# Blocks of head outputs in four tiles of their own, loaded inside the gates; second projection weights ahead in the load queue; bias rows copied from tile to tile

## The chip, the cores and the metric

One core of a Trainium2 chip runs the whole program. The metric is device time in microseconds; the time before is the median of three runs, 2127.23 us (2127.11 to 2127.78). A profiled execution of the same kernel has its own time, 2127.56 us, and its own span, 2125.8 us; the span is what the profile divides up.

## The reference

Two layers (DEPTH = 2) over 512 tokens of width 1024, all float32. In each layer one input projection feeds two branches, dilated window attention (output `y_a`, 384 wide) and retention (output `y_b`, 2048 wide: 4 heads of 512). The two are projected and merged by sigmoid gates, projected again, and followed by a SwiGLU feed-forward part; each sublayer ends in a layer norm.

```python
y_b = (jax.nn.silu(g_r) * y_r.reshape(B, S, RET_V_WIDTH)).astype(x.dtype)
merged = (jax.nn.sigmoid(gate_a) * jnp.einsum('bsc,cd->bsd', y_a, w_attn_proj)
          + jax.nn.sigmoid(gate_b) * jnp.einsum('bsc,cd->bsd', y_b, w_ret_proj))
return jnp.einsum('bsd,de->bse', merged, w_out)
```

## The kernel before

**Products.** Every float32 matrix is split into a high part (a cast on ScalarE, ACT) and a low part (the difference, on VectorE, DVE); `hilo` (L94) does both, `unit` (L123) does it for a weight tile of 128 x 1024, and a product is three matmuls: high by high, high by low, low by high. A matmul here streams 512 columns. Large products use seven block products instead of eight (`ORDER`, L313: A11·B11, A12·B21, S1·P1, S4·B22, S2·P2, S3·P3, A22·P4), where the S are sums of blocks of the left operand, split in the tile `xs`, and the P sums of weight blocks. A block product is 24 matmuls: two token tiles of 12.

**Loads.** Weights are loaded by `load` (L110) through the DMA queue of SyncE (SP) into one of eight shared buffers of 4 KB per partition, `raw` (L98); a buffer is free again when its two halves have been split. SP issues in order: a load that waits for a buffer holds up all loads behind it. Additions done by a DMA, and some loads and stores, go through GpSimd's (POOL's) queue, also in order.

**Order of work.** The program is written in one order, with a list `side` of small jobs handed out by `tick` between matmuls. The compiler then plans each engine's queue: an instruction written later can be put ahead of an earlier one on its engine when by the planner's own reckoning its inputs are ready first. On the chip each queue runs in that planned order, and an instruction that waits holds what stands behind it.

**The stretch that the change touches**, once per layer:
1. The last retention head's outputs are transposed and stored to DRAM as `y_d` (`turn`, L1038).
2. `gates(0)` and `gates(1)` (L1088) are two products of the layer's input with the gate weights: `left` makes `sga` tiles, `right` writes a sigmoid into a buffer `sb` (two of them) and stores it to `g_d`. The first block product of a chain is copied out of PSUM by ACT (`sn`, L496) before the next accumulates onto it.
3. During `gates(1)`, from its third block product, `side` holds `ya_put` (splits the attention output `yaT`) and `y_block` (loads two of the four blocks of `y_d`, heads 0 and 1, into `raw` buffers).
4. `was`: four weight units of the attention projection. Then `y_put` splits blocks (0, 0) and (0, 1) of `y_d` into `xh` and `xl`, the tiles that held the layer's input, and the two other blocks are loaded. `b11` is the first pair of weight tiles of the second (retention) projection.
5. Eight groups of nine matmuls are the attention projection; each is multiplied by its gate (`sg`, L1142) and stored to `g_d` by POOL. From the third group on the list `more` hands out `y_put(1, 1)` and the four sums `x_sums` (L208), which are done in place in the `y_d` blocks.
6. The retention projection (L1188 on): heads 0 and 1 by block products (`product`, L1213), heads 2 and 3 by plain ones (`plain`, L1223), four rounds of 24 matmuls with a weight tile each. The order is A11, A12, plain 0 to 3, S1 and so on. Four loads `yq` bring heads 2 and 3 from `y_d`; three are split into the tile `yp`, the fourth into a quarter of `xh` that is free. `u21` is the weight pair of A12. `p1` holds the sum B11 + B12: `p_load` loads the one and POOL adds the other (L1206).

**Memory.** Stage pools are stacked from two sides. On the right, after the shared buffers, stand `yap` (10 KB per partition: `yaT`, `cos`, `sin`) and later, in its place, `fin` (8 KB, the residual tile `xtok`) and `pp` (8 KB, `p1`); on the left stand the nine slots `opp` (36 KB) and `ret` (the retention tiles and `sb`), and later `m` (32 KB) and `yp` (24 KB). A tile waits for the last use of the tiles whose bytes it takes over.

At the very start, `bias_rows` (L462) gathers bias rows of both layers into a tile `rb`, twice: rows 0 to 15 and rows 32 to 47 hold the same values; the second copy becomes the low part.

Of the kernel before, what the change touches and what calls it, by code (L numbers as in the profile page):

```python
# [11 lines left out]
F32 = mybir.dt.float32  # L12
# [7 lines left out]
P = 128  # L20
S = 512
D = 1024
KD = D // P
NI = S // P
DEPTH = 2
# [30 lines left out]
def hybrid_kernel(ctx, tc, x, rel_bias, w_in, b_in, w_attn_proj, w_ret_proj, w_out,  # L56
# [23 lines left out]
    def stage(name, bufs=1, side="left"):  # L80
        return tc.tile_pool(name=name, bufs=bufs, side=side, reuse_waits="tile")
# [28 lines left out]
    def load(src, a, b):  # L110
        v = view(raw(), a, b)
        for v_, s_ in pieces(v, src):
            nc.sync.dma_start(v_, s_)
        return v
# [8 lines left out]
    def unit(v):  # L123
        a, b = v.shape[1], v.shape[2]
        h = view(wp.tile([P, 1024], F32R, tag="whi", name="whi"), a, b)
        l = view(wp.tile([P, 1024], F32R, tag="wlo", name="wlo"), a, b)
        hilo(v, h, l)
        return h, l
# [36 lines left out]
    def pace(us):  # L165
        rate[0], credit[0] = len(side) / us, 0.0

    def drain():
        while side:
            side.popleft()()  # L170
# [37 lines left out]
    def x_sums(cp):  # L208

        (a11, a12), (a21, a22) = cp  # L210

        def one(n, o_, a, b, op):
            dve.tensor_tensor(out=o_, in0=a, in1=b, op=op)  # L213
            t = xs[:, SN.index(n)]
            hilo(o_, t[:, 0], t[:, 1])

        return [lambda a=a: one(*a) for a in (("S1", a22, a21, a22, ALU.subtract), ("S3", a21, a11, a21, ALU.subtract),
                                              ("S2", a22, a22, a11, ALU.subtract), ("S4", a22, a22, a12, ALU.add))]
# [237 lines left out]
    def va_row(ly, t):  # L456
        return DEPTH * RH + 2 * ly + t

    def gate_row(ly, t):
        return DEPTH * (RH + 2) + 2 * ly + t  # L460

    def bias_rows():  # L462


        r = raw("rb")
        pool.memset(r, 0.0)
        for q in (0, BK):
            for ly in range(DEPTH):
                for b2 in range(2):
                    o, e = b2 * RV, (C_VR, C_GR)[b2]  # L470
                    pool.dma_start(r[q + ly * RH:q + (ly + 1) * RH, o:o + RV],
                                   b_in[ly, e:e + RH * RV].rearrange("(h n) -> h n", h=RH))
                    e = C_VA + 2 * b2 * VB
                    pool.dma_start(r[q + va_row(ly, 0):q + va_row(ly, 2), o:o + VB],
                                   b_in[ly, e:e + 2 * VB].rearrange("(h n) -> h n", h=2))
                    e = (C_GA, C_GB)[b2]
                    pool.dma_start(r[q + gate_row(ly, 0):q + gate_row(ly, 2), o:o + S],
                                   b_in[ly, e:e + D].rearrange("(h n) -> h n", h=2))

        def make():  # L480
            dve.tensor_tensor(out=r[:, RV:], in0=r[:, RV:], in1=r[:, :RV], op=ALU.add)
            act.copy(out=bh, in_=r)
            e = slice(BK, 2 * BK)
            dve.tensor_tensor(out=bh[e], in0=r[e], in1=bh[e].bitcast(F32), op=ALU.subtract)

        return make
# [197 lines left out]
    def layer(ly, cp):  # L684
# [6 lines left out]

        heads = [{} for _ in range(RH)]
        lay = ExitStack()
        yap = lay.enter_context(stage("yap", side="right"))
        yaT = yap.tile([P, NG, S], F32, name="yaT")
        opp = lay.enter_context(stage("opp", 9))
        csp = yap
# [294 lines left out]
                next(vg)  # L992
            drain()

        with stage("ret") as rp:
            def ret_scores(h):

                dec = rp.tile([P, S], F32, tag="dec", name="dec")
# [74 lines left out]
            wa_l, wr_l = rows(w_attn_proj[ly]), rows(w_ret_proj[ly])  # L1073
            y_v = rows(y_d)
            sga, ya, yb = [None] * NI, [], [[None, None], [None, None]]

            def ya_put(t):
                ya.append(slot("ya"))
                hilo(yaT[:, t], ya[t][:, 0], ya[t][:, 1])

            def y_block(a, b):
                yb[a][b] = load(y_v[:, 4 * b:4 * b + 4, a * 256:a * 256 + 256], 4, 256)

            def y_put(a, b):
                ks, ts_ = slice(4 * b, 4 * b + 4), slice(a * 256, a * 256 + 256)
                hilo(yb[a][b], xh[:, ks, ts_], xl[:, ks, ts_])

            def gates(c):  # L1088

                cs = slice(c * S, (c + 1) * S)  # L1090

                def left(i, ps, s):
                    if s is not None:
                        dve.tensor_tensor(out=s, in0=ps, in1=s, op=ALU.add)
                    if sga[i] is None:
                        sga[i] = slot("sg", F32)
                    act.activation(out=sga[i][:, c], in_=ps if s is None else s, func=AF.Sigmoid)

                def right(i, t):
                    sb = rp.tile([P, S], F32, tag="sb", name="sb", bufs=2)  # L1100
                    act.activation(out=sb, in_=t, func=AF.Sigmoid)
                    act.dma_start(g_d[1, i * P:(i + 1) * P, cs], sb)

                return biased(halves(w_l, 0, (2, 2), C_GA + c * S, C_GB + c * S, S), S, gate_row(ly, c), left, right)
# [3 lines left out]
            for n_, _ in enumerate(gates(1)):  # L1108
                if n_ == 2:
                    drain()  # L1110
                    side.extend([nothing] * 4 + [lambda t=t: ya_put(t) for t in range(NG)] + [lambda b=b: y_block(0, b) for b in range(2)])
                    pace(18)
            drain()

            def block_w(b, u):
                k = 4 * (b[1] == "2") + 2 * u
                c = (b[2] == "2") * S
                return wr_l[:, k:k + 2, c:c + S]
# [2 lines left out]
                return wr_l[:, 2 * RH + 2 * u:2 * RH + 2 * u + 2, hf * S:(hf + 1) * S]  # L1121

            was = [[unit(load(wa_l[:, o:o + n, hf * S:(hf + 1) * S], n, S)) for o, n in ((0, 2), (2, 1))] for hf in range(2)]
            for b in range(2):
                y_put(0, b)
            for b in range(2):
                y_block(1, b)
            more = [lambda: y_put(1, 1)] + x_sums(yb)
            b11 = [load(block_w("B11", u), 2, S) for u in range(2)]
            for hf in range(2):  # L1130
                if hf:
                    u11 = [unit(r) for r in b11]
                for i in range(NI):
                    ps = psum("ps")
                    ks = [(u, k) for u in was[hf] for k in range(u[0].shape[1])]
                    for t, ((h, l), k) in enumerate(ks):
                        yh, yl = (ya[t][:, e, i * P:(i + 1) * P] for e in range(2))
                        mm(ps, yh, h[:, k], t == 0, False)
                        mm(ps, yh, l[:, k], False, False)
                        mm(ps, yl, h[:, k], False, t == NG - 1)  # L1140
                    v = sga[i][:, hf]
                    dve.tensor_tensor(out=v, in0=v, in1=ps, op=ALU.mult)  # L1142
                    pool.dma_start(g_d[0, i * P:(i + 1) * P, hf * S:(hf + 1) * S], v)
                    if hf * NI + i >= 2 and more:
                        more.pop(0)()
        lay.close()

        fin = ExitStack()
        fp = fin.enter_context(stage("fin", side="right"))
        xt = [fp.tile([P, 2, D], F32, name="xtok")]  # L1150
        res = (x if ly == 0 else spill).rearrange("(h i p) d -> h p i d", p=P, h=2)
        pool.dma_start(xt[0], res[0])

        def xtok(i):
            return xt[i // 2][:, i % 2]
# [32 lines left out]
        with stage("mp") as mp:  # L1188
# [4 lines left out]
            with stage("yp") as ypp, stage("pp", side="right") as ppp:  # L1193
# [66 lines left out]
                        act.copy(out=t, in_=ps)  # L1260
                    return ts

                yq = [load(y_v[:, 8 + 2 * q:10 + 2 * q], 2, S) for q in range(4)]
                u21 = [unit(load(block_w("B21", u), 2, S)) for u in range(2)]
                while more:
                    more.pop(0)()
                for q, r in enumerate(yq[:3]):
                    hilo(r, yp[:, 0, 2 * q:2 * q + 2], yp[:, 1, 2 * q:2 * q + 2])
                hilo(yq[3].rearrange("p e (h t) -> p (e h) t", h=2), xh[:, 0:4, 256:S], xl[:, 0:4, 256:S])
                for u in range(2):  # L1270
                    p_load(u, "B11", False)
                for u in range(2):
                    p_load(u, "B12", True)

                A = pair()
                product("A11", u11, A, True)
                ahead = unit(load(plain_w(0, 0), 2, S))
                sn1 = copies(A)
                X = pair()
                product("A12", u21, X, True)  # L1280
                Y = pair()
                for u in range(4):
                    now = ahead
                    if u < 3:
                        ahead = unit(load(plain_w(u + 1, 0), 2, S))
                    else:
                        for i in range(2):
                            g_load(i, 0)
                        ahead = p_units()
                    plain(u, now, X + Y)  # L1290
# [28 lines left out]
                    dve.tensor_tensor(out=sn5[a], in0=sn5[a], in1=Z[a], op=ALU.add)  # L1319
                now, ahead = ahead, [unit(r) for r in p3]  # L1320
                product("S2", now, A, False)
                sn6 = copies(A)
                for a in range(2):
                    dve.tensor_tensor(out=sn6[a], in0=C[a], in1=sn6[a], op=ALU.subtract)
# [251 lines left out]
```

## Time and profile before

| what | us |
|---|---|
| median of three runs | 2127.23 |
| profiled execution: its time / its span | 2127.56 / 2125.8 |
| TensorE (PE) busy in the span | 2091.5 |
| layer 0: last matmul of A11 / first of A12 | 590.56 / 595.64 |
| layer 1: last matmul of A11 / first of A12 | 1645.13 / 1650.52 |

In the lists below a timeline row is: start, duration, engine, line, operation, tiles written and read, shapes, and in brackets the idle time of that engine just before with what ended it. A row of waits is: engine, tile and line that waited, what it waited for, then microseconds in total, how many times, and the longest. A row of DMA issues ends in the KB of one transfer and the median us from issue to landing. A row of stretches gives, after its window, the busy time of PE, weight loads, DVE, ACT and POOL, then the granted PE clock, the share of the DMA engines' time and GB/s.

### The profile page before, as it was taken

How to read it: one execution, taken by the hardware profiler on the slowest of the kernel's cores; microseconds unless marked ns; L12 is line 12 of the kernel's file. 1: busy time of each engine (PE TensorE's matmuls, PEld its weight loads, DVE VectorE, ACT ScalarE, POOL GpSimd, SP SyncE). 2: the span in 40 equal slices, each digit the busy share in tenths (PEclk: the TensorE clock that was granted, in tenths of full speed). 3: DMA queues.
4: the chain of work that ended last, by engine and by line, in shares of the span. 5: the costliest groups of instructions: out<-in, count | busy, mean ns of one | idle time of the engine just before them, and what ended most of it. 6: DMA issues, size and time to landing. Idle time of an engine off the chain costs nothing. (4 is left out here: it accounts for less than half of the span.)

```text
span 2125.8 us, 33803 instructions
## 1 busy us (share of the span) xinstructions
PE 2091.5 (98%) x13178; PEld 1867.7 (88%) x13178; DVE 1623.9 (76%) x2327; ACT 1129.2 (53%) x1725; POOL 285.6 (13%) x299
## 2 busy tenths in 40 slices
PE   8999999999989999999999999999999999999998
PEld 7989888888778898999899898888887789989897
DVE  7666888786756698887787578887766567988876
ACT  5567655555543265555355765555654433655551
POOL 4111111110110101111030111111001111110111
PEclk9999999999999999999999999999999999999999
DMA  7866567676887458868258555758667873687771
GB/s 231 214 172 142 135 150 183 178 181 164 242 254 231 113 140 201 195 156 231 80 156 221 151 126 135 193 136 216 165 178 246 252 225 79 162 198 186 183 198 46
DMA packets 303905, 374.37 MB, mean 176 GB/s; under 512 B 23277, under 2 KB 208785, under 8 KB 303616
## 3 DMA queue, kind: packets, MB, share of 16 engines
q1 hardware_dynamic: 213056, 259.30, 39.5%
q0 software_dynamic: 63280, 100.11, 25.3%
q10 hardware_dynamic: 27408, 12.80, 2.1%
q8 instruction: 103, 1.69, 0.3%
q14 instruction: 58, 0.48, 0.1%
HBM read 346.36 MB, written 28.53 MB: 176 GB/s over the span
## 5 line engine op out<-in xcount | busy, mean ns | idle before, releaser
L351 DVE TENSOR_TENSOR wlo<-raw,whi 128x1024 fp32r<-128x1024 f32 (+1 forms) x518 | 605.0, 1171 | 200.5 <-ACT whi L345 186.3
L345 ACT CAST whi<-raw 128x1024 fp32r<-128x1024 f32 (+1 forms) x518 | 519.8, 1007 | 442.2 <-PE ps L84 188.9
L84 PE MATMUL ps<-xs,whi 128*128 128x256 f32 x2176 | 399.5, 284 | 0.4 <-ACT sn L813 0.4
L84 PE MATMUL ps<-whi,xs 128*128 128x512 f32 (+1 forms) x1152 | 348.2, 372 | 5.7 <-ACT sn L496 5.7
L84 PEld LDWEIGHTS ps<-xs,whi 128*128 128x128 f32 x2176 | 339.4, 192 | 4.9 <-issue 1.7
L84 PE MATMUL ps<-xh,whi 128*128 128x256 f32 (+1 forms) x1104 | 318.4, 290 | 2.2 <-ACT xh L95 1.9
L84 PE MATMUL ps<-xl,whi 128*128 128x256 f32 (+1 forms) x1104 | 315.5, 286 | 0.0
L84 PE MATMUL ps<-xh,wlo 128*128 128x256 f32 (+1 forms) x1104 | 315.1, 286 | 0.0
L84 PE MATMUL ps<-xs,wlo 128*128 128x256 f32 x1088 | 308.0, 283 | 2.6 <-DVE wlo L351 2.6
L84 PEld LDWEIGHTS ps<-whi,xs 128*128 128x128 f32 x1152 | 209.9, 188 | 40.8 <-ACT sn L496 6.8
L84 PEld LDWEIGHTS ps<-xh,whi 128*128 128x128 f32 x1104 | 210.4, 191 | 10.2 <-ACT xh L95 3.4
L84 PEld LDWEIGHTS ps<-xl,whi 128*128 128x128 f32 x1104 | 211.4, 192 | 3.0 <-DVE xl L96 0.6
L84 PE MATMUL ps<-wlo,xs 128*128 128x512 f32 (+1 forms) x576 | 212.9, 370 | 0.1
L84 PEld LDWEIGHTS ps<-xh,wlo 128*128 128x128 f32 x1104 | 211.2, 191 | 1.5
L84 PEld LDWEIGHTS ps<-xs,wlo 128*128 128x128 f32 x1088 | 208.5, 192 | 3.2 <-DVE wlo L351 3.2
L336 POOL DMA_DIRECT2D raw<-in_w_in x80 | 97.4, 1239 | 692.3 <-DMA raw<-in_w_in 290.6
L84 PE MATMUL ps<-whi,xh 128*128 128x512 f32 (+1 forms) x464 | 177.2, 382 | 9.7 <-ACT whi L95 9.7
L367 DVE TENSOR_TENSOR raw<-raw 128x1024 f32<-128x1024 f32 (+1 forms) x148 | 173.9, 1175 | 6.9 <-DMA raw<-in_w_in 4.9
L84 PE MATMUL ps<-wlo,xh 128*128 128x512 f32 (+1 forms) x464 | 174.3, 376 | 1.4 <-DVE wlo L96 1.4
L84 PE MATMUL ps<-whi,xl 128*128 128x512 f32 (+1 forms) x464 | 173.8, 375 | 0.0
L84 PE MATMUL ps<-whi,ht 128*128 128x512 f32 x544 | 170.1, 391 | 0.0
L95 ACT CAST whi<-raw 128x1024 fp32r<-128x1024 f32 (+1 forms) x78 | 76.0, 983 | 108.7 <-PE ps L84 79.6
(241 smaller groups left out, 3322.9 us busy)
## 6 DMA issues: line engine op xcount, KB each, us to landing
raw<-in_w_in SPq DMA_DIRECT2D x168, 512.0 KB, 5.2
raw<-in_w_in POOLq DMA_DIRECT2D x64, 512.0 KB, 8.7
raw<-in_w_ffn_up SPq DMA_DIRECT2D x64, 512.0 KB, 4.9
raw<-in_w_ffn_down SPq DMA_DIRECT2D x52, 512.0 KB, 4.7
raw<-in_w_ffn_gate SPq DMA_DIRECT2D x44, 512.0 KB, 4.9
raw<-in_w_ffn_gate POOLq DMA_DIRECT2D x40, 512.0 KB, 7.5
raw<-in_w_ret_proj SPq DMA_DIRECT2D x32, 512.0 KB, 5.9
raw<-in_w_in SPq DMA_DIRECT2D x56, 256.0 KB, 4.9
```

Of the source, the lines that this page charges most:

```text
L84: pe.matmul(ps, lhsT=a, rhs=b, start=start, stop=stop, skip_group_check=True)
L95: act.copy(out=hi, in_=src)
L336: pool.dma_start(r, self.src({"P1": "B12", "P3": "B22"}[n], u), accum_op=ALU.add)
L345: act.copy(out=h, in_=src)
L351: dve.tensor_tensor(out=l, in0=src, in1=h.bitcast(F32), op=ALU.subtract)
L367: dve.tensor_tensor(out=r, in0=r, in1=self.t["B22" if n == "P2" else "B21", u], op=ALU.add)
```

## The change

- The four blocks of heads 0 and 1 get tiles of their own (`yr00` to `yr10`, 16 KB on the right side), and all four loads are issued by one job, `y_blocks`, in the middle of `gates(1)`. For that the pools `yap` and `ret` are closed at that point, and `gates(1)`'s sigmoids get a pool `sbp` of four buffers in place of two.
- After `gates(1)` a copy of two elements per partition on ACT reads the sigmoid tile of the second token tile of block product S2 and writes into `xh`, in the two blocks that `y_put(0, 0)` and `y_put(0, 1)` overwrite.
- `b11` and `b21`, the weight pairs of A11 and A12, are loaded straight after `was`; the sums keep their order S1, S3, S2, S4, and S4 is written after the eight groups instead of inside them.
- The residual load into `xtok` moves from before the retention projection to after its S2 product.
- Of the `yq` loads two are issued ahead, with the first plain weight tile between them; the others follow one per plain round, and so do their splits. The `p_load`s are written after A11 instead of before it.
- `bias_rows` loads the rows once, and one DMA copies rows 0 to 15 of the tile to rows 32 to 47.

```diff
-        for q in (0, BK):
-            for ly in range(DEPTH):
-                for b2 in range(2):
...
+        for ly in range(DEPTH):
+            for b2 in range(2):
+                o, e = b2 * RV, (C_VR, C_GR)[b2]
+                pool.dma_start(r[ly * RH:(ly + 1) * RH, o:o + RV],
+                               b_in[ly, e:e + RH * RV].rearrange("(h n) -> h n", h=RH))
...
+        pool.dma_start(r[BK:BK + NR], r[:NR])
...
-        yap = lay.enter_context(stage("yap", side="right"))
+        yas, ret = ExitStack(), ExitStack()
+        yap = yas.enter_context(stage("yap", side="right"))
...
-        with stage("ret") as rp:
+        with ret:
+            rp = ret.enter_context(stage("ret"))
...
+            sbp, sbs, yrs = [rp, 2], [], ExitStack()
...
-            def y_block(a, b):
-                yb[a][b] = load(y_v[:, 4 * b:4 * b + 4, a * 256:a * 256 + 256], 4, 256)
+            def y_blocks():
+                yas.close()
+                ret.close()
+                sbp[:] = lay.enter_context(stage("sbp")), 4
+                yr = yrs.enter_context(stage("yr", side="right"))
+                for a, b in ((0, 0), (0, 1), (1, 1), (1, 0)):
+                    yb[a][b] = yr.tile([P, 4, 256], F32, name=f"yr{a}{b}")
+                    nc.sync.dma_start(yb[a][b], y_v[:, 4 * b:4 * b + 4, a * 256:a * 256 + 256])
...
-                    sb = rp.tile([P, S], F32, tag="sb", name="sb", bufs=2)
+                    sb = sbp[0].tile([P, S], F32, tag="sb", name="sb", bufs=sbp[1])
+                    sbs.append(sb)
...
-                    side.extend([nothing] * 4 + [lambda t=t: ya_put(t) for t in range(NG)] + [lambda b=b: y_block(0, b) for b in range(2)])
-                    pace(18)
+                    side.extend([nothing] + [lambda t=t: ya_put(t) for t in range(NG)] + [y_blocks])
+                    pace(9)
             drain()
+            act.copy(out=xh[:, 0:8:4, 0:1], in_=sbs[-3][:, 0:2].unsqueeze(2))
...
+            b11, b21 = ([load(block_w(n, u), 2, S) for u in range(2)] for n in ("B11", "B21"))
             for b in range(2):
                 y_put(0, b)
-            for b in range(2):
-                y_block(1, b)
-            more = [lambda: y_put(1, 1)] + x_sums(yb)
-            b11 = [load(block_w("B11", u), 2, S) for u in range(2)]
+            s1, s3, s2, s4 = x_sums(yb)
+            more = [lambda: y_put(1, 1), s1, s3, s2]
...
+            s4()
         lay.close()
+        yrs.close()
...
-        pool.dma_start(xt[0], res[0])
...
-                yq = [load(y_v[:, 8 + 2 * q:10 + 2 * q], 2, S) for q in range(4)]
-                u21 = [unit(load(block_w("B21", u), 2, S)) for u in range(2)]
-                while more:
-                    more.pop(0)()
-                for q, r in enumerate(yq[:3]):
-                    hilo(r, yp[:, 0, 2 * q:2 * q + 2], yp[:, 1, 2 * q:2 * q + 2])
-                hilo(yq[3].rearrange("p e (h t) -> p (e h) t", h=2), xh[:, 0:4, 256:S], xl[:, 0:4, 256:S])
+                yq, pq = [yq_load(0)], [load(plain_w(0, 0), 2, S)]
+                yq.append(yq_load(1))
+                u21 = [unit(r) for r in b21]
+                yq_put(0, yq[0])
+                A = pair()
+                product("A11", u11, A, True)
                 for u in range(2):
                     p_load(u, "B11", False)
                 for u in range(2):
                     p_load(u, "B12", True)
-
-                A = pair()
-                product("A11", u11, A, True)
-                ahead = unit(load(plain_w(0, 0), 2, S))
+                ahead = unit(pq[0])
                 sn1 = copies(A)
                 X = pair()
                 product("A12", u21, X, True)
                 Y = pair()
                 for u in range(4):
                     now = ahead
+                    if u < 2:
+                        yq.append(yq_load(u + 2))
                     if u < 3:
                         ahead = unit(load(plain_w(u + 1, 0), 2, S))
+                        yq_put(u + 1, yq[u + 1])
...
                 product("S2", now, A, False)
+                pool.dma_start(xt[0], res[0])
```

More of the change, by code (lines that the diff above doesn't have):

```diff
@@ L466, in bias_rows @@
         pool.memset(r, 0.0)
-        for q in (0, BK):
-            for ly in range(DEPTH):
-                for b2 in range(2):
[L470 to L478, printed above, removed]
+        for ly in range(DEPTH):
[3 more added lines that the diff above has]
+                               b_in[ly, e:e + RH * RV].rearrange("(h n) -> h n", h=RH))
+                e = C_VA + 2 * b2 * VB
+                pool.dma_start(r[va_row(ly, 0):va_row(ly, 2), o:o + VB],
+                               b_in[ly, e:e + 2 * VB].rearrange("(h n) -> h n", h=2))
+                e = (C_GA, C_GB)[b2]
+                pool.dma_start(r[gate_row(ly, 0):gate_row(ly, 2), o:o + S],
+                               b_in[ly, e:e + D].rearrange("(h n) -> h n", h=2))
+        pool.dma_start(r[BK:BK + NR], r[:NR])
         def make():
@@ L1261, in copies, with yq_load, yq_put @@
                     return ts
-                yq = [load(y_v[:, 8 + 2 * q:10 + 2 * q], 2, S) for q in range(4)]
-                u21 = [unit(load(block_w("B21", u), 2, S)) for u in range(2)]
-                while more:
-                    more.pop(0)()
-                for q, r in enumerate(yq[:3]):
-                    hilo(r, yp[:, 0, 2 * q:2 * q + 2], yp[:, 1, 2 * q:2 * q + 2])
-                hilo(yq[3].rearrange("p e (h t) -> p (e h) t", h=2), xh[:, 0:4, 256:S], xl[:, 0:4, 256:S])
+                def yq_load(q):
+                    return load(y_v[:, 8 + 2 * q:10 + 2 * q], 2, S)
+                def yq_put(q, r):
+                    if q < 3:
+                        hilo(r, yp[:, 0, 2 * q:2 * q + 2], yp[:, 1, 2 * q:2 * q + 2])
+                    else:
+                        hilo(r.rearrange("p e (h t) -> p (e h) t", h=2), xh[:, 0:4, 256:S], xl[:, 0:4, 256:S])
+                yq, pq = [yq_load(0)], [load(plain_w(0, 0), 2, S)]
[4 more added lines that the diff above has]
+                product("A11", u11, A, True)
                 for u in range(2):
```

## The prediction

> **What bounds the kernel now.** I read the page first, for which engine is full.
>
> ```profile
> span 2125.8 us, 33803 instructions
> ...
> PE 2091.5 (98%) x13178; PEld 1867.7 (88%) x13178; DVE 1623.9 (76%) x2327; ACT 1129.2 (53%) x1725; POOL 285.6 (13%) x299
> ```
>
> TensorE (PE) is busy for 98% of the span. The change takes no matmul away, so it can gain only time in which PE stands still or runs slowly. The second view is the list of what PE waited for.
>
> ```profile
> PE ps L84 <- ACT whi L95: 9.7, 2, 5.0
> PE ps L84 <- ACT sn L496: 5.7, 3, 3.3
> ...
> PE ps L84 <- ACT xh L95: 1.9, 5, 1.0
> ```
>
> Two waits, one in each layer, make 9.7 us: a weight tile split at L95. The next row is a wait for a copy out of PSUM in the biased products (L496). Third comes PE's timeline around these waits; first layer 0, then layer 1.
>
> ```profile
> 548.01 0.39 PE L84 MATMUL ps<-whi,xs 128*128 128x512 f32 x1
> 549.73 0.50 PE L84 MATMUL ps<-whi,xs 128*128 128x512 f32 x1 [1.33 <-ACT sn L496]
> ...
> 590.56 0.39 PE L84 MATMUL ps<-whi,xl 128*128 128x512 f32 x1
> 595.64 0.76 PE L84 MATMUL ps<-whi,xh 128*128 128x512 f32 x1 [4.69 <-ACT whi L95]
> ...
> 597.50 0.63 PE L84 MATMUL ps<-whi,xl 128*128 128x512 f32 x1
> 597.93 0.63 PE L84 MATMUL ps<-whi,xh 128*128 128x512 f32 x1
> ...
> 604.88 0.61 PE L84 MATMUL ps<-whi,yp 128*128 128x512 f32 x2
> 606.10 0.50 PE L84 MATMUL ps<-wlo,yp 128*128 128x512 f32 x1 [0.60 <-DVE wlo L96]
> ```
>
> ```profile
> 1600.69 0.39 PE L84 MATMUL ps<-whi,xs 128*128 128x512 f32 x1
> 1604.34 0.50 PE L84 MATMUL ps<-whi,xs 128*128 128x512 f32 x1 [3.25 <-ACT sn L496]
> 1604.67 0.39 PE L84 MATMUL ps<-wlo,xs 128*128 128x512 f32 x1
> 1604.90 0.63 PE L84 MATMUL ps<-whi,xs 128*128 128x512 f32 x2
> ...
> 1645.13 0.39 PE L84 MATMUL ps<-whi,xl 128*128 128x512 f32 x1
> ...
> 1659.94 0.61 PE L84 MATMUL ps<-whi,yp 128*128 128x512 f32 x2
> ```
>
> Matmuls overlap, so I count from start to start. From 549.73 to 590.56 PE starts 179 further matmuls (one token tile of S4, then S2, S3 and A22, eight groups of nine, A11): 40.83 / 179 = 0.228 us each. After the hole at 590.56 the step is 0.43 (597.50 to 597.93), nearly twice as long, so the hole costs more than its own length. After the shorter one at 1600.69 the step is 0.23 at once (1604.67 to 1604.90).
>
> What holds PE up stands on ACT and in SP's load queue (layer 0):
>
> ```profile
> 547.20 1.05 ACT L95 CAST xh<-raw 128x1024 fp32r<-128x1024 f32 x1 [3.87 <-DMA raw<-y_d]
> ...
> 549.10 0.58 ACT L496 COPY sn<-ps 128x512 f32<-128x512 f32 x1
> ...
> 561.68 0.63 ACT L1101 ACTIVATE sb<-sn 128x512 f32<-128x512 f32 x1 [0.46 <-DVE sn L500]
> ...
> 589.78 1.05 ACT L95 CAST xh<-raw 128x1024 fp32r<-128x1024 f32 x1 [11.07 <-DMA raw<-y_d]
> ...
> 594.55 1.04 ACT L95 CAST whi<-raw 128x1024 fp32r<-128x1024 f32 x1 [2.77 <-DMA raw<-in_w_ret_proj]
> ```
>
> ```profile
> 540.76 3.27 SPq L113 DMA_DIRECT2D raw<-y_d  x2
> ...
> 561.08 2.10 SPq L113 DMA_DIRECT2D raw<-y_d  x2
> 565.12 1.57 SPq L113 DMA_DIRECT2D raw<-in_w_ret_proj  x2
> ...
> 573.19 7.39 SPq L113 DMA_DIRECT2D raw<-y_d  x4
> 581.36 18.36 SPq L113 DMA_DIRECT2D raw<-in_w_ret_proj  x6
> ```
>
> In the gates the copy that PE needs (549.10) stands on ACT behind the split of a `y_d` block (547.20) that waits for its load. At A12 the weights B21 come last in the queue, from 581.36 on, behind eight `y_d` loads; ACT is held 11.07 us by the last of these, then still waits 2.77 us for the weights.
>
> **The change part by part.**
>
> *B21 ahead in the queue, the `y_d` blocks out of the shared buffers.* The four block loads give back four buffer turns, and the two loads of 561.08 no longer stand ahead of B11. So B11 can take the place of 561.08, and B21 that of 565.12, 16 us earlier than 581.36. Two windows of DMA issues show what such a load took, the first from 580 to 583 us, the second from 560 to 575 us:
>
> ```profile
> raw<-in_w_ret_proj SPq DMA_DIRECT2D x1, 512.0 KB, 13.1
> ```
>
> ```profile
> raw<-in_w_ret_proj SPq DMA_DIRECT2D x2, 512.0 KB, 5.4
> ```
>
> Issued by 567 and landing by 573, or by 580 at the worst 13.1, B21 is there before A12 at 590.8. The hole goes, with its slow stretch: normally A12's 24 matmuls and the step to the next take 25 x 0.228 = 5.70 us; they took 604.88 - 590.56 = 14.32 in layer 0 and 1659.94 - 1645.13 = 14.81 in layer 1. Gain 8.62 + 9.11 = 17.73 us. The first plain weight tile, now loaded ahead too, also ends the wait at 606.10: 1.22 for two steps of 0.46 together, gain 0.76.
>
> *The two-element copy.* It makes the splits of blocks (0, 0) and (0, 1) wait for the sigmoid of 561.68, which comes after the PSUM copies that PE needs; the split can no longer stand ahead of 549.10. Gain 549.73 - 548.01 - 0.23 = 1.49 in layer 0, 1604.34 - 1600.69 - 0.23 = 3.42 in layer 1. The copy itself is not in the trace; between nothing and the 0.58 us of a 512-column copy, on an ACT with 11 us to spare: I take nothing. It is queued behind ACT's own sigmoid, so it adds no wait for another engine.
>
> *What the moved splits cost.* They now fall into DVE's fullest stretch, here with one row for its load and rows for its kinds of work:
>
> ```profile
> 562.00:590.60 28.60, 28.60 (x128) 23.46 (x126) 18.90 (x22) 11.45 (x15) 6.33 (x9) 1.00 0.93 296
> ```
>
> ```profile
> 583.58 0.68 DVE L1142 TENSOR_TENSOR sg<-sg,ps 128x512 f32<-128x512 f32 x1
> 590.86 1.23 DVE L96 TENSOR_TENSOR xl<-raw,xh 128x1024 fp32r<-128x1024 f32 x1 [6.60 <-ACT xh L95]
> ...
> 593.74 1.22 DVE L213 TENSOR_TENSOR raw<-raw 128x1024 f32<-128x1024 f32 x1
> ```
>
> DVE is busy 18.90 of 28.60 us. Due before A12 are now also two block splits, the low part of S2, S4's sum and low part and two low parts of B21: seven of 1.23 and one `sg` of 0.68, 9.3 us. Two attention weight splits go out, since their loads take the buffers of 540.76 (1.9 us). That makes 26.3 of 28.6: it fits, with small waits likely where DVE waits in order. Bounds: 0, or up to the 2.4 of S4 per layer if S4 goes ahead of B21; I take 1.0 per layer, 2.0 in all.
>
> *The rest costs nothing while covered.* Four `sb` buffers: ACT waits fall away, none of which PE waited for. The residual load, moved past S2, is needed only at the output projection. The `p_load`s now wait for the blocks' memory, until S4's sum; P1 is due only after A11, A12 and four plain rounds, 33 us after A11 begins; a late S4 is the last rival below. The bias rows:
>
> ```profile
> L477 POOL DMA_DIRECT2D rb<-in_b_in x8: 511/511/511, 6.8 to 21.8; - x8
> ...
> L481 DVE TENSOR_TENSOR rb<-rb x1: 682/682/682, 30.9 to 30.9; 128x512 f32<-128x512 f32 x1
> ...
> DMA to landing us min/median/max: 2.7/5.2/5.8
> ```
>
> Twelve issues of 0.5 us end by about 14, their landing by 20, and a copy as slow as the slowest row (5.8) lands at 26, before DVE reads at 30.9. Loss 0, and 1.9 us (all PE waits for `xh`) bounds what a freer start could gain; I take 0.
>
> **The sum.** 17.73 + 0.76 + 1.49 + 3.42 = 23.40 gained, 2.0 given back: 21.4. The profiled execution took 2127.56 us (span 2125.8 and 1.76 around it), 0.33 over the median of the runs. From the median: 2127.2 - 21.4 = **2105.8 us**.
>
> **The rivals.**
>
> *The gate wait changes hands.* With `y_d` out of the way the planner may put an attention weight split ahead of the copy of 549.10, and its load now stands behind four block loads in SP's queue. For: in both layers the planner set a split there whose load was late. Against: these loads need no `y_d`. If it stays as long as now: 2105.8 + 4.91 = 2110.7.
>
> *The hole moves to the first plain product.* `yp` takes over the memory of a gate slot and must wait for that slot's store:
>
> ```profile
> 594.12 0.54 POOL L1143 DMA_DIRECT2D g_d<-sg  x1 [9.02 <-DVE sg L1142]
> ```
>
> ```profile
> g_d<-sg POOLq DMA_DIRECT2D x1, 256.0 KB, 4.7
> ```
>
> If it is the last store and that stays where it is, it lands at 598.8, and after a cast (1.05) plain 0 starts at 599.9 instead of 590.8 + 24 x 0.228 = 596.3: 3.6 us. Against: the last `sg` was late only because DVE stood behind ACT's wait of 11.07. The hole lies between 3.25 (no slow stretch) and 4.69 (a slow one), so the rows alone give 3.6, or with a slow stretch 3.6 + 3.9 (8.62 - 4.69), per layer: 2109.4 for one layer to 2120.8 for two. The Trainium skill (TensorE: Matmul & The Clock Gate, Part 1: The HAM clock gate) puts the threshold at an idle window of about 3.4 us, after which the clock is halved until PE has been busy about as long; the steps of 0.43 after 4.69 us and 0.23 after 3.25 agree. By that rule this hole would cost the full 7.5 per layer.
>
> *The change doesn't reach B21.* If too few buffers come free and B21 still goes at 581.36, the hole stays and only the gates' part is gained: 2127.2 - 4.9 + 2.0 = 2124.3, no change by this measure.
>
> *Slower.* SP issues in order, and the `p_load`s wait there until S4 has left the blocks' memory; behind them stand the weights for plain 1, due at 596.3 + 5.5 = 601.8. If S4's sum stays at 593.74, they go at about 596 and, at 13.1 us, land at 609; with both splits 611.4, a hole of 9.6 and a slow stretch of 3.9, in each layer: 2105.8 + 27.0 = 2132.8. It decides from a hole of 6.8 us per layer on (2 x 10.7 = 21.4). Against: S4 was late through the same ACT wait, which goes.
>
> **How the numbers follow.** Forecast 0.70, gate wait 0.10, first plain product 0.09, B21 not reached 0.05, slower 0.06. The forecast's own range is 2127.2 - 23.4 - 1.9 = 2101.9 to 2105.8 + 2.8 (DVE at its bound) = 2108.6. Taking in the gate rival and a plain hole in one layer (2113.3 with its slow stretch) I set 2101.9 to 2114. What can be told from no change is about 0.2%, 4.3 us: faster means below 2123.0, slower above 2131.5. Faster 0.70 + 0.10 + 0.09 = 0.89, same 0.05, slower 0.06.
>
> **What would show it.** Right: no row "PE ps L84 <- ACT whi L95" of 5 us, A12's start one step behind A11's end, no step of 0.43 there, the gates' wait for L496 below 1 us, B21 issued before the eight groups begin. Wrong: a new hole at plain 0 or 1, an ACT wait on an attention weight load inside the gates, or SP held at the `p_load`s into the 590s.

## The result, and the profile after

| | median us | range | runs |
|---|---|---|---|
| before, beside it | 2127.78 | 2127.11 to 2132.28 | 5 |
| after | 2106.83 | 2104.53 to 2107.93 | 5 |
| after, once more beside the experiments | 2103.74 | 2101.74 to 2105.01 | 4 |

The ratio is 0.9894 with a 95% interval of 0.988 to 0.9908, so about 21 us or 1.1% faster; the forecast was 2105.8. The third row is the same kernel on a later occasion (ratio 0.9879, 0.9859 to 0.9899). Its median is 3 us lower, so differences of 3 us between kernels that did not run side by side mean nothing below.

First, the head of the page of the changed kernel.

```profile
span 2105.1 us, 33783 instructions
...
PE 2084.9 (99%) x13178; PEld 1863.1 (89%) x13178; DVE 1622.4 (77%) x2327; ACT 1127.8 (54%) x1727; POOL 279.9 (13%) x288
```

The span is 20.7 us shorter, but PE's busy time fell by only 6.6 us (2091.5 to 2084.9). The rest was standing still. Part of the busy time went too, because the slow matmuls behind the holes counted as busy. The list of PE's waits shows what is left.

```profile
PE px L1260 <- DVE raw L1253: 2.7, 2, 1.3
PE ps L84 <- ACT sn L496: 2.1, 2, 1.2
```

The row of 9.7 us for a weight split at L95 is gone, and the longest wait for L496 fell from 3.3 to 1.2 us. At the head of the list is a wait that was not there before: transposes at L1260, once in each layer, for a product on DVE at L1253. In PE's timeline the old places are closed and the new one is open:

```profile
546.91 0.61 PE L84 MATMUL ps<-whi,xs 128*128 128x512 f32 x2
...
587.71 0.39 PE L84 MATMUL ps<-whi,xl 128*128 128x512 f32 x1
587.94 0.39 PE L84 MATMUL ps<-whi,xh 128*128 128x512 f32 x1
...
619.35 0.39 PE L84 MATMUL ps<-whi,xs 128*128 128x512 f32 x1
621.07 0.66 PE L1260 MATMUL px<-ident,raw 128*128 128x128 f32 x4 [1.33 <-DVE raw L1253]
...
1590.45 0.62 PE L84 MATMUL ps<-whi,xs 128*128 128x512 f32 x2
...
1631.25 0.39 PE L84 MATMUL ps<-whi,xl 128*128 128x512 f32 x1
1631.48 0.39 PE L84 MATMUL ps<-whi,xh 128*128 128x512 f32 x1
```

The rows at 546.91 and 1590.45 hold the two matmuls between which PE used to wait in the gates. A12 starts 0.23 us after A11's last matmul in both layers (587.71 to 587.94, 1631.25 to 1631.48), one normal step.

Both traces hold the same 13178 matmuls, in the same order but for two that change places in each layer, so the difference of their start times can be followed along the run. This table shows where it changes (after minus before, us):

```text
start of the run up to 97 us                  -1.10
gates, layer 0                                -1.49
A22, layer 0                                  -0.26
A12 and its slow steps, layer 0               -8.63
first plain weight tile, layer 0              -0.78
first gated transposes (L1260), layer 0       +1.70
1594 us                                       +0.30
gates, layer 1                                -3.40
A12 and its slow steps, layer 1               -9.22
S1, layer 1                                   +0.31
first gated transposes (L1260), layer 1       +1.53
later gated transposes, layer 1               +0.32
end                                          -20.7
```

### The profile page after: what moved, and what is told of

Read it like the earlier page. It is cut to its first block, busy times and chain, and to the rows that moved or that the text cites. A ratio compares the mean times of both kernels' runs of the same rounds, so it can differ in the third digit from the quotient of the medians.

```text
span 2105.1 us, 33783 instructions
## 1 busy us (share of the span) xinstructions
PE 2084.9 (99%) x13178; PEld 1863.1 (89%) x13178; DVE 1622.4 (77%) x2327; ACT 1127.8 (54%) x1727; POOL 279.9 (13%) x288
## 4 chain that ended last, share of the span: by engine, by line
PE 83%; DVE 5%; issue 5%; DMA 4%; ACT 2%; POOL 1%; ACTq 0%; SPq 0%; POOLq 0%; DVEq 0%
PE ps L84 74%; PE px L84 6%; DMA p<-in_w_ret_proj 2%; DMA raw<-in_w_in 1%; DVE wlo L351 1%; PE px L582 1%; ACT whi L345 1%; PE px L1044 1%; DVE wlo L96 1%; PE px L193 1%; DMA g_d<-sb 1%; DVE xs L96 0%; DVE sg L1153 0%; DVE yr L213 0%; PE px L1260 0%
## 5 line engine op out<-in xcount | busy, mean ns | idle before, releaser
L95 ACT CAST whi<-raw 128x1024 fp32r<-128x1024 f32 (+1 forms) x78 | 76.0, 984 | 100.5 <-PE ps L84 57.4
```

Of the source, the lines that this page charges most:

```text
L95: act.copy(out=hi, in_=src)
```

## The experiments

**The two-element copy taken out.** It was predicted to be what clears the gates.

```diff
-            act.copy(out=xh[:, 0:8:4, 0:1], in_=sbs[-3][:, 0:2].unsqueeze(2))
```

> The changed kernel without the two-element copy behind the gates. Theory A (the blocks of y_d now arrive after the gates' last copies out of PSUM, so no split can stand ahead of them; the copy does nothing): time as the changed kernel, 2106.8 within 1 us, and the gates' wait for L496 stays at 2.1 us over two waits with none above 1.2. Theory B (the prediction's step: the copy is what holds the splits back): the two gate waits come back, 1.49 + 3.42 = 4.9 us, time 2111.7, a wait for L496 above 3 us in layer 1.

Measured: 2103.1 us (2101.3 to 2104.37), lower than either theory said, though the changed kernel itself, run again later, took 2103.74. PE's list has one wait for L496:

```profile
PE ps L84 <- ACT sn L496: 0.8, 1, 0.8
```

The gates stay clean, so theory A holds: in the changed kernel the copy does nothing. ACT's timeline shows why, first that of the changed kernel, then that of the kernel without the copy:

```profile
555.60 0.58 ACT L496 COPY sn<-ps 128x512 f32<-128x512 f32 x1
...
558.63 0.19 ACT L1125 CAST xh<-sb 128x2 fp32r<-128x2 f32 x1 [0.41 <-ACT sb L1112]
...
564.50 1.05 ACT L95 CAST xh<-yr 128x1024 fp32r<-128x1024 f32 x1 [2.82 <-DMA yr<-y_d]
```

```profile
554.99 0.58 ACT L496 COPY sn<-ps 128x512 f32<-128x512 f32 x1
...
563.59 1.05 ACT L95 CAST xh<-yr 128x1024 fp32r<-128x1024 f32 x1 [2.54 <-DMA yr<-y_d]
```

With or without it, the planner puts the first block split behind the gates' last copies out of PSUM and the split starts at about 564, where it waits for its load.

**The copy alone, in the kernel before.** Only two sigmoid buffers are there, so it reads the last but one.

```diff
+                    sbs.append(sb)
...
+            act.copy(out=xh[:, 0:8:4, 0:1], in_=sbs[-2][:, 0:2].unsqueeze(2))
```

> The kernel before with the two-element copy alone (it reads the third sigmoid tile instead of the second, since only two buffers are there), blocks of y_d still in shared buffers. Theory A (a copy that the splits must wait for is enough to clear the gates where the blocks arrive early; in the changed kernel it is idle because the blocks arrive late there): the gate waits for L496 go, 4.9 us gained by 1605 us of the run; behind them the splits free their buffers 10 us later, so the A12 hole stays or grows by up to 3 us per layer: 2123 to 2129. Theory B (the copy never had an effect): the gate waits stay at 1.3 and 3.3 us, 2127.8 within 1 us.

Measured: 2121.09 us (2118.4 to 2124.52), ratio 0.9957 (0.994 to 0.9973), below the range of theory A. Against the profile of the kernel before, the gates gain 1.25 us in layer 0 and 3.39 in layer 1, and the hole at A12 stays:

```profile
PE ps L84 <- ACT whi L95: 9.6, 3, 5.4
...
PE ps L84 <- ACT sn L496: 1.3, 2, 0.8
```

On ACT the first split of a block now starts behind the copy, where it stood at 547.20 before:

```profile
563.54 1.03 ACT L95 CAST xh<-raw 128x1024 fp32r<-128x1024 f32 x1
```

So theory A holds in kind: the copy clears the gates where blocks arrive early, and is idle where they arrive late. The median lies 7.7 us below that of the kernel before beside it (2128.82), 3 us more than the gates give; the profiled execution is the slowest of the four (2124.52), and where the others gain more is not shown.

**B21 ahead alone, in the kernel before.** The blocks of `y_d` stay in shared buffers.

```diff
-            b11 = [load(block_w("B11", u), 2, S) for u in range(2)]
+            b11, b21 = ([load(block_w(n, u), 2, S) for u in range(2)] for n in ("B11", "B21"))
...
-                u21 = [unit(load(block_w("B21", u), 2, S)) for u in range(2)]
+                u21 = [unit(r) for r in b21]
```

> The kernel before, with the B21 loads alone moved to directly behind those of B11; blocks of y_d still in shared buffers. Theory A (B21 came late because it stood in the queue behind four loads of y_d that waited for buffers): B21 takes the first two buffers that come free from 573 us on, lands by 583 to 589, A12 starts within 2 us of A11's end in each layer, the gate waits (4.9) stay: 2127.8 - 17.7 = 2110, up to 2113 with the 2 us. Theory B (the buffers themselves are what is missing: four blocks of y_d hold half of the eight until the sums are done): B21 comes free no earlier than 579, a hole of over 3 us stays at A12 in at least one layer, or moves to plain 0: 2118 to 2128.

Measured: 2131.71 us over 10 runs, ratio 1.0022 (1.0013 to 1.0032): this half of the change is a small loss. SP's queue, ACT and PE of this kernel:

```profile
570.87 0.98 SPq L113 DMA_DIRECT2D raw<-in_w_ret_proj  x2
576.21 5.55 SPq L113 DMA_DIRECT2D raw<-y_d  x4
585.48 12.74 SPq L113 DMA_DIRECT2D raw<-in_w_ret_proj  x4
```

```profile
594.58 1.04 ACT L95 CAST xh<-raw 128x1024 fp32r<-128x1024 f32 x1 [9.79 <-DMA raw<-y_d]
...
599.79 1.04 ACT L95 CAST whi<-raw 128x1024 fp32r<-128x1024 f32 x1
```

```profile
600.88 1.65 PE L84 MATMUL ps<-whi,yp 128*128 128x512 f32 x3 [6.62 <-ACT whi L95]
603.84 0.80 PE L84 MATMUL ps<-wlo,yp 128*128 128x512 f32 x1 [1.31 <-DVE wlo L96]
```

B21 goes at 570.87 instead of 581.36 and A12 runs without a hole. But the two buffers are now missing for heads 2 and 3: their four loads go from 576.21 instead of 573.19, in a kernel that is 2 us ahead of the kernel before. ACT waits 9.79 us for a `y_d` load, the plain weight's cast stands behind it (599.79; its own load, issued at 585.48, took 10.4 us), and PE waits 6.62 us at the first plain product, and that round's 24 matmuls, the wait of 1.31 among them, take 10.4 us at the slow clock instead of 24 x 0.228 = 5.5. Theory B holds in its mechanism. The time lies above its range, which ended at 2128: it named a hole of over 3 us, and the hole that moved is 6.62 us with a slow round behind it. The same hole is in layer 1 (6.44 us).

**The tiles alone.** From the changed kernel the copy and the whole new order are taken out; the four tiles, the early closing of the pools, the four `sb` buffers, S4's place, the later residual load and the bias rows stay, so "alone" means without copy and order.

```diff
-            act.copy(out=xh[:, 0:8:4, 0:1], in_=sbs[-3][:, 0:2].unsqueeze(2))
...
-            b11, b21 = ([load(block_w(n, u), 2, S) for u in range(2)] for n in ("B11", "B21"))
+            b11 = [load(block_w("B11", u), 2, S) for u in range(2)]
...
+                yq = [load(y_v[:, 8 + 2 * q:10 + 2 * q], 2, S) for q in range(4)]
+                u21 = [unit(load(block_w("B21", u), 2, S)) for u in range(2)]
...
+                for u in range(2):
+                    p_load(u, "B11", False)
...
                 A = pair()
                 product("A11", u11, A, True)
+                ahead = unit(load(plain_w(0, 0), 2, S))
```

> The changed kernel with the queue order of the second projection undone: B21, the four yq loads, the plain weights and the p loads are written as before, and the two-element copy is out; left of the change are the four tiles of their own, the early closing of the pools, the four sigmoid buffers, S4's place, the bias rows. Theory A (free buffers alone are enough): B21 is issued before 575, no hole at A12, gates clean: 2106 to 2109. Theory B (the order is needed too): B21 waits behind the yq loads into the 580s, a hole of 3 to 5 us at A12 per layer with its slow steps: 2118 to 2124.

Measured: 2107.22 us (2106.07 to 2111.37), ratio 0.9914 (0.9893 to 0.9935). SP's queue and PE's timeline:

```profile
562.22 3.25 SPq L113 DMA_DIRECT2D raw<-y_d  x3
568.85 20.57 SPq L113 DMA_DIRECT2D raw<-in_w_ret_proj  x6
```

```profile
597.03 0.50 PE L84 MATMUL ps<-wlo,yp 128*128 128x512 f32 x1 [2.08 <-DVE wlo L96]
...
598.38 0.63 PE L84 MATMUL ps<-whi,yp 128*128 128x512 f32 x1
598.81 0.63 PE L84 MATMUL ps<-wlo,yp 128*128 128x512 f32 x1
...
1640.58 0.50 PE L84 MATMUL ps<-wlo,yp 128*128 128x512 f32 x1 [1.94 <-DVE wlo L96]
```

B21 is issued from 568.85, though it is written behind the `y_d` loads, and A12 starts on time in both layers: with the tiles, enough buffers are free for every load. Theory A holds. What the order adds is the first plain weight tile, late here by 2.08 and 1.94 us. Its load is not what is late: the two loads behind those of B21 were issued by 581 and took 4.9 us. On ACT and DVE the splits of heads 2 and 3, which the order spreads over the plain rounds, stand ahead of its split:

```profile
594.63 1.21 DVE L96 TENSOR_TENSOR xl<-raw,xh 128x1024 fp32r<-128x1024 f32 x1
595.76 4.62 DVE L96 TENSOR_TENSOR wlo<-raw,whi 128x1024 fp32r<-128x1024 f32 x4
```

Against the changed kernel's first profile that place costs 4.1 us of start time in layer 0 with its slow steps, and 1.7 of them come back at the transposes, where PE, now later, no longer waits; the end lies only 0.7 us behind. But that profile is of another occasion. Beside this kernel ran the one without the copy, which has the whole order: 2103.1 us (2101.3 to 2104.37) against 2107.22 (2106.07 to 2111.37); their profiles lie 5.2 us apart, 1.1 of it at the start. So the order is worth about 4 us, and what stays without it the larger part, about 20 (2127.69 to 2107.22).

**The bias rows alone, in the kernel before.** Its edit is the first hunk of the change.

```diff
-        for q in (0, BK):
-            for ly in range(DEPTH):
...
+        for ly in range(DEPTH):
...
+        pool.dma_start(r[BK:BK + NR], r[:NR])
```

> The kernel before with the bias rows edit alone. The changed kernel stood 1.1 us ahead of the kernel before by 97 us. Theory A (the bias rows did this, through fewer issues on POOL and what the planner makes of them): matmul for matmul this kernel is 1.1 us ahead of the kernel before by 97 us and 1.1 from there to the end. Theory B (chance of one execution: the first transposes ran at half clock in one profile and not in the other): it differs from the kernel before by less than 0.3 us at 97 us, or by another amount than 1.1.

Measured: one execution, 2124.4 us, 1.19 us ahead of the kernel before at 97 us, which looks like theory A, though by the end it is 3.2 us ahead and not 1.1. Two other comparisons overturn it. The kernels with B21 ahead and with the copy alone, whose start is that of the kernel before, are 2.02 and 1.18 us ahead at the same place; and the changed kernel run twice differs from itself by 1.27 us at 94 us. The start varies by that much from execution to execution, and no gain of the bias rows can be told from it.

**The new wait.** Three kernels ran beside the changed kernel as a control.

> The changed kernel unaltered, as the control for the runs beside it. All theories: 2106.8 within 2 us; the wait of the first gated transposes for L1253 is 0.5 to 1.4 us in each layer (1.3 and 1.3 in the first profile, 1.0 and 0 with the two-element copy out).

Measured: 2103.74 us, below the range expected; the wait is 1.8 us over both layers, as expected. The suspected chain is in the changed kernel's chain of waits (start, us, what the time went to; pieces of it), and SP's queue shows what stands ahead of P1's loads there:

```profile
587.76 1.22 DVE yr L213
...
591.70 8.68 DMA p<-in_w_ret_proj
...
601.30 13.17 DMA p<-in_w_ret_proj x2
...
614.57 1.06 ACT whi L95
...
616.79 1.22 DVE wlo L96
618.01 0.67 DVE sn L1312 x2
...
619.13 1.29 DVE raw L1252 x2
620.41 0.61 DVE raw L1253
...
621.07 0.66 PE px L1260 x4
```

```profile
578.67 0.37 SPq L113 DMA_DIRECT2D raw<-in_w_ret_proj  x1
...
585.60 2.64 SPq L113 DMA_DIRECT2D raw<-in_w_ret_proj  x2
590.14 1.50 SPq L113 DMA_DIRECT2D raw<-g_d  x2
591.70 0.97 SPq L1220 DMA_DIRECT2D p<-in_w_ret_proj  x2
```

S4's sum, in the blocks whose memory is taken over, is done at 588.98 (587.76 + 1.22). P1's loads go at 591.70, behind two loads of gates that SP held for buffers until 591.28. Load and additions last until 614.47, beside the residual load of 1 MB that POOL issues at 592.68:

```profile
592.68 0.72 POOL L1342 DMA_DIRECT2D xtok<-in_x  x1 [7.41 <-DVE xs L96]
```

Then the splits of P1 go through ACT and DVE. PE hardly waits for P1 itself (0.2 us in its list of waits). But behind the splits, in DVE's order, stand the sums and gate products (L1312, L1252, L1253) that the transposes need, and so these are late. Two ways to test it. In the first, the residual load is held back by one element written into its tile; the load overwrites it.

```diff
+                act.copy(out=xt[0][:, 0, 0:1], in_=sn5[0][:, 0:1])
                 pool.dma_start(xt[0], res[0])
```

> The changed kernel with the residual load (1 MB) held back behind the fifth block product by a one-element copy. Theory A (P1 is late because its two loads share the DMA engines with the residual load, 9.6 us from issue to landing): the loads land about 2 us sooner, the second P1 split ends by 615 instead of 616.9, and the wait of the first gated transposes goes: 2.7 us less than the control. Theory B (P1 is late because its loads are issued late; other transfers fill the DMA engines anyway): the loads still take 7 us or more and the time is the control's within 0.7 us.

In the second, P1's loads are made early as well.

```diff
-                for a, b in ((0, 0), (0, 1), (1, 1), (1, 0)):
+                for a, b in ((0, 0), (1, 0), (0, 1), (1, 1)):
                     yb[a][b] = yr.tile([P, 4, 256], F32, name=f"yr{a}{b}")
+                for a, b in ((0, 0), (0, 1), (1, 1), (1, 0)):
                     nc.sync.dma_start(yb[a][b], y_v[:, 4 * b:4 * b + 4, a * 256:a * 256 + 256])
...
-                        nc.sync.dma_start(p1[u], block_w(b, u))
+                        pool.dma_start(p1[u], block_w(b, u))
...
+                act.copy(out=xt[0][:, 0, 0:1], in_=sn5[0][:, 0:1])
```

> The changed kernel with P1's loads early: the block tiles are placed so that p1 lies over the blocks (0, 0) and (1, 0), which are free after S2's sum (583.2) instead of S4's (592.4), the two loads go through POOL's queue, free of SP's, and the residual load is held back as in the run beside it. Theory A (late issue of P1's loads makes the new wait): they go by 586, the second P1 split ends by 612, the wait of the first gated transposes for L1253 goes in both layers: 2.7 to 3.4 us less than the control. Theory B (the wait is DVE's own order or load, not P1): P1 early changes nothing there, the time is the control's within 0.7 us.

And the same without the two-element copy:

> The same with the two-element copy out as well. Theory A (the copy does nothing): the time of the run with P1 early within 1 us. Theory B (the copy costs something: without it the changed kernel took 2103.1, with it 2106.8, measured on different occasions): 2 to 4 us less than the run with P1 early.

| | median us | range | wait of the transposes for the gate product |
|---|---|---|---|
| control | 2103.74 | 2101.74 to 2105.01 | 1.8 over both layers |
| residual load held back | 2101.19 | 2100.21 to 2103.01 | none |
| P1 early | 2103.12 | 2100.29 to 2103.99 | none |
| P1 early, no copy | 2102.48 | 2101.7 to 2103.04 | none |

The rows that decide are first PE's list of waits of the control, then DVE's and PE's timelines of the kernel with P1 early (where the gate product stands at L1254 and the transposes at L1261):

```profile
PE px L1260 <- DVE raw L1253: 1.8, 2, 1.2
```

```profile
607.60 1.23 DVE L96 TENSOR_TENSOR wlo<-p,whi 128x1024 fp32r<-128x1024 f32 x1 [2.75 <-ACT whi L95]
...
613.91 1.37 DVE L1313 TENSOR_TENSOR sn<-ps,sn 128x512 f32<-128x512 f32 x2 [1.09 <-PE ps L84]
...
616.40 1.28 DVE L1254 TENSOR_TENSOR raw<-raw 128x512 f32<-128x512 f32 x2
```

```profile
619.83 0.60 PE L1261 MATMUL px<-ident,raw 128*128 128x128 f32 x4
```

With P1 early its second split ends at 608.83, DVE's sum now waits for PE (1.09) instead of the other way round, and both gate products are done at 617.7, 2.1 us before the first transposes. In matmul start times this place gains 0.72 us in layer 0 and 1.41 in layer 1 against the control (1.53 and 1.64 against the changed kernel's first profile). So theory A holds for the wait. It does not hold for the time: 0.6 us below the control, within the spread; in the two profiled executions the start was 1.9 us slower than the control's at 94 us. The row of waits is the evidence, and the time alone would have spoken for theory B. (The expectation's 592.4 is the end of S4's split, which did not hold P1's loads: they went at 591.70.)

Holding the residual load back took the wait away by itself (0.57 and 1.36 us against the control), there with little to spare: its gate products end at 617.8 (616.53 + 1.29) and the transposes start at 617.93. Its median is 2.6 us below the control's, but the ranges overlap. As the kernel with P1 early holds the residual load back too, no run tests the early issue by itself. What the two kernels share is that P1's second split is done earlier, at 613.08 and 608.83 against 614.48 in the control, with the same work behind it in DVE's order: late P1 made the wait, and how much of the lateness is SP's queue and how much the load's duration is not separated. Whether the residual load as such is to blame stays open: P1's loads took 9.9, 9.7 and 9.6 us in three profiles with it alongside, but 8.2 and 7.6 in the kernel without the copy and the one with the tiles alone, which have it too, and 8.3 with it held back.

```profile
p<-in_w_ret_proj SPq DMA_DIRECT2D x4, 512.0 KB, 9.9
```

```profile
p<-in_w_ret_proj SPq DMA_DIRECT2D x4, 512.0 KB, 8.3
```

(The changed kernel, then the one with the residual load held back; the last number is the median us from issue to landing.) Taking the copy out of the kernel with P1 early changes nothing that can be told (2102.48 against 2103.12): theory A again.

**Two sigmoid buffers instead of four**, one execution:

```diff
-                sbp[:] = lay.enter_context(stage("sbp")), 4
+                sbp[:] = lay.enter_context(stage("sbp")), 2
```

> The changed kernel with two sigmoid buffers instead of four. Theory A (the four buffers cost and gain nothing): 2103 to 2107, no wait of TensorE for L496 above 1.5 us. Theory B (they help clear the gates): a wait for L496 of 3 us or more appears in one of the layers.

Measured: 2104.87 us; PE's row of waits for L496:

```profile
PE ps L84 <- ACT sn L496: 1.5, 2, 1.1
```

Theory A, as far as one execution can tell: the four buffers cost and gain nothing here.

## Why the prediction was right, and where not

- **The hole at A12** (17.73 us predicted) measured 8.63 + 9.22 = 17.85. The step named two edits together, B21 ahead and the blocks out of the shared buffers. The runs split it: the tiles without the order close the hole, B21 ahead alone moves it to the first plain product and loses.
- **The gates** (1.49 and 3.42) measured 1.49 and 3.40, but the cause was named wrongly. The step said the two-element copy keeps the split from standing ahead of the PSUM copy. In the changed kernel, taking the copy out changes nothing; the splits come late there because the blocks' loads go late. `y_blocks` is written in the middle of the gates, yet its loads go at 557.66, in SP's queue behind weights that were written later:

```profile
551.08 6.27 SPq L113 DMA_DIRECT2D raw<-in_w_ret_proj  x3
557.66 3.07 SPq L1092 DMA_DIRECT2D yr<-y_d  x4
```

SP was held there by buffers for these weights until 556.98, and only the last 0.2 us were a wait for the store of a sigmoid, whose memory a new tile takes over. That the planner put the loads so late because of this store is likely, but no run moves them earlier to show it. Part of the size may be chance: in the profiled execution of the kernel with the bias rows alone, whose gates are those of the kernel before, the two gate waits were 0.6 and 1.3 us shorter.
- **The first plain weight tile** (0.76) measured 0.78 in layer 0. The kernel with the tiles alone shows that more hangs on it: without that order this tile is 2 us late in both layers.
- **The moved splits in DVE's fullest stretch** (2.0 given back) cost nothing that the trace shows; PE has no wait there. Elsewhere twice as much was given back, 4.2 us: 1.70 and 1.53 at the gated transposes, and 0.9 in small steps. The step that failed is the one that called the `p_load`s free while covered. It measured their cover against PE's need of P1, 33 us after A11 begins, and there PE hardly waits. Missing was what stands behind P1's second split in DVE's order: from its end at 616.88 DVE works until 621.03 on a weight split, the sums and the gate products, and the transposes could have started at about 619.6, one step behind the matmul at 619.35. That the sum came out near is partly luck: 2.2 us more lost than forecast stand against 1.4 us gained that nobody forecast, 1.10 at the start and 0.26 in A22.
- **Bias rows, four `sb` buffers** (0): no effect that could be told. The start was 1.10 us better in the first profile, no more than the same kernel differs from itself.
- **The rivals.** The gate wait did not change hands. The hole at plain 0 did not come here, but it did in two experiments, once behind late `y_d` loads and once behind the splits of heads 2 and 3; neither trace shows a wait for `yp`'s memory there. B21 was reached. The slower rival's mechanism is there in a small form: SP issues the `p_load`s only at 591.70, after S4. But S4's sum was done at 589.0 instead of 595, the weights of plain 1 to 3 stood ahead of the `p_load`s in SP's queue (578.67 and 585.60) and not behind, and the price fell on DVE.

## What to carry to other kernels

In this kernel a buffer shortage wasn't cured by a better queue order: the load moved ahead took its buffer from the next ones, and the hole moved with it. With enough buffers the order was still worth about 4 us. Count the buffers first and order the queue second. When a load gets later, follow its consumer's queue: not only when the loaded tile is needed, but what stands behind its split on the in-order engine and who waits for that. And a small guard for the planner should be tried by taking it out, since another edit may already do its work.

## What the runs showed of the hardware that was not expected

- The slow clock doesn't follow from a hole's length alone. In the kernel with the tiles alone an idle time of 2.08 us in layer 0 was followed, 1.35 us after its end, by steps of 0.43 (598.38 to 598.81), which last until 601.4. An idle time of 2.29 us in the gates of the kernel with B21 ahead (layer 1) had such steps, too. But 1.94 us at the same place of layer 1 in the kernel with the tiles alone had none, and neither had 2.16 us in the gates of the kernel with the bias rows alone, nor the 3.25 us in the kernel before. The Trainium skill (TensorE: Matmul & The Clock Gate, Part 1: The HAM clock gate) has the clock halved after at least one idle window of about 3.4 us; the row of 2.08 us differs from that, and the measurement decides. The page also says that the window runs freely, and that the same kernel therefore varies from run to run. That would let two holes of like length differ, but a whole window of 3.4 us does not fit into an idle time of 2.08, and no run here shows the window itself.
- The first 97 us of one and the same kernel differ by 1.27 us between two executions, so a start-up edit of 1 us can't be judged from one profile.
